# A two-level fast matmul with Gelu, 4096 x 4096 x 4096: more products split a second time, A staged in longer runs and weighed on the way

## The chip, the core and the metric

One NeuronCore of a Trainium2 chip. TensorE multiplies, VectorE (DVE) adds and transposes, ScalarE (ACT) copies out of PSUM, squares and applies Gelu, GpSimd (POOL) and SyncE (SP) issue the transfers. The metric is device time in microseconds; before the change the median of three runs is 1574.81 us (1572.47 to 1576.79).

## The reference

```python
def setup_inputs():
    m, k, n = 4096, 4096, 4096
    return {"a": np.random.randn(m, k).astype(np.float32),
            "b": np.random.randn(k, n).astype(np.float32)}

def reference(a, b):
    x = np.matmul(a, b)
    return 0.5 * x * (1 + np.tanh(np.sqrt(2 / np.pi) * (x + 0.044715 * x**3)))
```

## The kernel before

The product is made by a scheme of Strassen's kind. A, B and the output are cut into quadrants "11", "12", "21", "22" of 2048 x 2048, the operands are converted to 16 bit while they are loaded, and seven products M1 to M7 of sums of quadrants stand for eight. A group is one block of 512 rows of each A half (mb) with one block of 512 columns of each B half (nb): 16 groups, 0 to 15, four to each mb, each of 7 products of 64 matmuls (128 x 128 by 128 x 512). A's block changes during groups 3, 7 and 11. In the first six groups ("raw") B is loaded from the input (converted on the way) and its sums are kept in DRAM (`k_M`); later groups fetch those, in units of 1 MB, into a ring of 8 places in SBUF (`bK`). Group 0 does the first half of K with eight plain products, since nothing else is loaded yet.

Products, and the second level: a "split" product is itself cut into quarters and made of seven quarter products of 256 columns (112 narrow matmuls in place of 64 wide ones). Two consecutive products are split together, with their quarter products interleaved (`PAIR`). Quarter sums of B are made once by VectorE and kept in DRAM (`k_split`); those of A are made when needed, from block sums (`aD`).

```python
PRODUCTS = [
    ("M3", "Y", "11", ("12", "22", 1)),
    ("M5", "X", ("11", "12", -1), "22"),
    ("M7", "X", ("12", "22", -1), ("21", "22", 1)),
    ("M1", "X", ("11", "22", -1), ("11", "22", -1)),
    ("M4", "X", "22", ("21", "11", 1)),
    ("M2", "Y", ("22", "21", -1), "11"),
    ("M6", "Y", ("21", "11", -1), ("11", "12", 1)),
]
...
FRESH = [PRODUCTS[k] for k in (0, 1, 2)] + [
    ("M2", "Y", ("21", "22", -1), "11"), PRODUCTS[3], ("M4", "Y", "22", ("21", "11", 1)),
    ("M6", "X", ("21", "11", -1), ("11", "12", 1)),
]
NP = len(PRODUCTS)
QPH = 4
...
MAKES = (("M3", (1, 0)), ("M5", (2, 1)), ("M1", (4, 0)), ("M2", (5, 3)))
M3_M5, M2_M1 = 0, 3
PLACE = {"M3": (M3_M5, 0), "M5": (M3_M5, 1), "M2": (M2_M1, 0), "M1": (M2_M1, 1)}
SPLIT_AHEAD = 6
FETCH_AHEAD = 12
SPLITS = {M3_M5: (11, 13, 14, 15), M2_M1: (13, 14)}
LOAD_AHEAD = 6
CHECK_GROUP = 9

TURNS = ((2, 2), (3, 3), (5, 2), (6, 2), (8, 0), (9, 0), (10, 2), (11, 2))
```

`SPLITS` says which groups split the pair that begins at product 0 (M3 and M5) and at product 3 (M2 and M1). `FRESH` is the order of products of groups that split the second pair. `TURNS` are the steps at which the staged chunks of the next A block are transposed.

Staging of A: `load_a` fetches a chunk into one of two `stage` buffers, `turn_a` transposes it on VectorE into `aT`, `weigh_rows` sums the squares of its rows on ScalarE. These sums (and those of B, from `square`) decide at the end whether the 16-bit scheme stands or a general path must run. Block 0 of A is loaded a second time, around groups 9 to 12, for its sums alone.

```python
    def load_a(mb, quad, c, h=None):

        ih, kh = int(quad[0]) - 1, int(quad[1]) - 1
        n = NX if h is None else NX // 2
        x = 0 if h is None else h * n
        x0 = (ih * MH + mb * TM) // Q + x
        if not h:
            s = pool.tile([P, NX, RUN], F16, name="stage", tag="stage", bufs=2)
            staged[mb, quad, c] = s
        s = staged[mb, quad, c]
        return [
            (s[g * Q : (g + 1) * Q, x : x + n, :], a_v[kh * CH + c, g, :, x0 : x0 + n, :])
            for g in range(4)
        ]

    def turn_a(mb, quad, c, h=None):
        if not h:
            t = pool.tile([P, NJ // 2, TM * 2], F16, name="aT", tag=f"aT{a_slot[quad]}{c}")
            a_tiles[mb, quad, c] = t
        s, t = staged[mb, quad, c], a_tiles[mb, quad, c]
        x = slice(0, NX) if h is None else slice(h * NX // 2, (h + 1) * NX // 2)
        src = s.bitcast(U32).rearrange("p mb (jj q) -> p jj mb q", q=Q)
        dst = t.bitcast(U32).rearrange("p jj (mb q) -> p jj mb q", q=Q)
        nc.vector.transpose(dst[:, :, x, :], src[:, :, x, :])
        if h != 0 and mb == 0:
            del staged[mb, quad, c]
...
    def weigh_rows(mb, quad, c, xs):

        ih, kh = int(quad[0]) - 1, int(quad[1]) - 1
        s = staged[mb, quad, c]
        if (mb, ih) not in weighed:
            weighed[mb, ih] = pool.tile([P, 2 * CH, NX], F32, name="rows", tag="rows")
        if xs[0] == 0:
            weighed[mb, quad, c] = pool.tile([P, RUN], BF16, name="scrap", tag="scrap")
        for x in xs:
            k = kh * CH + c
            nc.scalar.activation(
                weighed[mb, quad, c][:, :RUN], s[:, x, :], ACT.Square, accum_out=weighed[mb, ih][:, k, x : x + 1]
            )
        if xs[-1] == NX - 1:
            del weighed[mb, quad, c], staged[mb, quad, c]

    def weigh_half(mb, ih):
        k, t = next(checks["a"]), weighed.pop((mb, ih))
        nc.vector.tensor_reduce(
            out=stats["a"][:, k * NX : (k + 1) * NX],
            in_=t.rearrange("p k x -> p x k"), axis=AX.X, op=ALU.add,
        )
...
    def stage_block(mb, turns, turned=True):
        def do(n, fn, *args):
            before.setdefault(n, []).append((fn, args))

        free_at = [0, 0]
        for (quad, c), n in zip(chunks, turns):
            do(max(n - LOAD_AHEAD, free_at.pop(0)), load, (load_a, (mb, quad, c)))
            free_at.append(n + 4)
            if turned:
                do(n, turn_a, mb, quad, c)
            for x in range(3):
                do(n + 1 + x, weigh_rows, mb, quad, c, list(range(NX))[x * 6 : (x + 1) * 6])
            if c == CH - 1 and quad in ("12", "21"):
                do(n + 4, weigh_half, mb, int(quad[0]) - 1)

    for gi in range(len(groups) - 1):
        if groups[gi + 1][0] != groups[gi][0]:
            stage_block(groups[gi + 1][0], [step_number(gi, s, q) for s, q in TURNS])
    stage_block(0, [first_step[CHECK_GROUP] + 8 + 6 * x for x in range(len(chunks))], turned=False)
```

What happens to a finished product, in normal order (`keep` is an ACT copy from PSUM, `tt` a VectorE operation on two tiles, `emit` the Gelu and the output transfer, `new_y` one of five buffers):

```python
        elif name == "M1":
            post["x1", i] = keep("x1", X, RT)
            later.append((gi, i))
        elif name == "M4":
            if not end:
                emit(gi, i, 0, 0, new_y(), X)
            x1 = post["x1", i]
            tt(x1, X, x1, ALU.add)
        elif name == "M2":
            y = new_y()
            tt(y, post.pop(("x1", i)), Y, ALU.subtract)
            if gi:
                flush()
            waiting.append((gi, i, 1, 0, y, y))
        elif name == "M6":
            y = new_y()
            tt(y, Y, post.pop(("x7", i)), ALU.add)
            flush()
            waiting.append((gi, i, 1, 1, y, y))
```

The plan of a split group (cut):

```python
            block = q in SPLIT and not isinstance(oa, str)
            if block and q == PAIR[0][1]:
                places[s] = [ring_place(n, SPLIT_AHEAD, (gi, s, c)) for c in range(CH)]
                users[s] = []
                e = max(ready, last_a, *(e for _, e in places[s]))
                for c, (x, _) in enumerate(places[s]):
                    task(e, open_block, gi, s, c, x)
                for qq in range(QPH):
                    task(e, block_sum, gi, s, oa, qq)
                last_a = e
            o = SPLIT[q][1] if q in SPLIT else oa
            e = n
            if not isinstance(o, str):
                ahead = SPLIT_AHEAD if q in SPLIT else AHEAD
                only = any(n - ahead <= x <= n for x in makes) or made and q not in SPLIT
                tag = "aS" if only or n_a % 2 else "bS"
                n_a += 1
                e = max(n - ahead, ready, last_a, free[tag][-AHEAD - 1] + 1)
                assert e <= n, steps[n]
                free[tag].append(n)
                last_a = e
                task(e, operand_a, gi, s, q, tag)
```

Of the kernel before, what the change touches and what calls it, by code (L numbers as in the profile page):

```python
# [16 lines left out]
P = 128  # L17
Q = 32
# [27 lines left out]
]  # L46
NP = len(PRODUCTS)
# [15 lines left out]

MAKES = (("M3", (1, 0)), ("M5", (2, 1)), ("M1", (4, 0)), ("M2", (5, 3)))
M3_M5, M2_M1 = 0, 3
PLACE = {"M3": (M3_M5, 0), "M5": (M3_M5, 1), "M2": (M2_M1, 0), "M1": (M2_M1, 1)}
SPLIT_AHEAD = 6
FETCH_AHEAD = 12
SPLITS = {M3_M5: (11, 13, 14, 15), M2_M1: (13, 14)}
LOAD_AHEAD = 6  # L70
CHECK_GROUP = 9

TURNS = ((2, 2), (3, 3), (5, 2), (6, 2), (8, 0), (9, 0), (10, 2), (11, 2))
# [8 lines left out]
N_PLAIN = 2 * len(PLAIN)  # L82
N_WARM = 46
# [48 lines left out]
def half_path(  # L132
# [26 lines left out]
    checks = {which: iter(range(stats[which].shape[1] // NX)) for which in stats}  # L159

    a_v = a.rearrange("(x mm) (c g r) -> c g mm x r", mm=Q, g=4, r=RUN)
    b_v = b.rearrange("(c g jj q e) n -> c g e q jj n", g=4, q=Q, e=2, jj=NJ // 2)
# [6 lines left out]
    def load_a(mb, quad, c, h=None):  # L169
# [5 lines left out]
        if not h:  # L175
# [4 lines left out]
            (s[g * Q : (g + 1) * Q, x : x + n, :], a_v[kh * CH + c, g, :, x0 : x0 + n, :])  # L180
# [3 lines left out]
    def turn_a(mb, quad, c, h=None):  # L184
        if not h:
            t = pool.tile([P, NJ // 2, TM * 2], F16, name="aT", tag=f"aT{a_slot[quad]}{c}")
            a_tiles[mb, quad, c] = t
        s, t = staged[mb, quad, c], a_tiles[mb, quad, c]
        x = slice(0, NX) if h is None else slice(h * NX // 2, (h + 1) * NX // 2)
        src = s.bitcast(U32).rearrange("p mb (jj q) -> p jj mb q", q=Q)  # L190
        dst = t.bitcast(U32).rearrange("p jj (mb q) -> p jj mb q", q=Q)
        nc.vector.transpose(dst[:, :, x, :], src[:, :, x, :])  # L192
        if h != 0 and mb == 0:
            del staged[mb, quad, c]

    def load_b(nb, quad, c, h=None):
        kh, jh = int(quad[0]) - 1, int(quad[1]) - 1
        n0 = jh * NH + nb * NC
        if not h:
# [5 lines left out]
            (t[g * Q : (g + 1) * Q, e::2, :], b_v[kh * CH + c, g, e, :, :, n0 : n0 + NC])  # L205
# [23 lines left out]
    def weigh_rows(mb, quad, c, xs):  # L229

        ih, kh = int(quad[0]) - 1, int(quad[1]) - 1
        s = staged[mb, quad, c]
        if (mb, ih) not in weighed:
            weighed[mb, ih] = pool.tile([P, 2 * CH, NX], F32, name="rows", tag="rows")
        if xs[0] == 0:
            weighed[mb, quad, c] = pool.tile([P, RUN], BF16, name="scrap", tag="scrap")
        for x in xs:
            k = kh * CH + c
            nc.scalar.activation(  # L239
                weighed[mb, quad, c][:, :RUN], s[:, x, :], ACT.Square, accum_out=weighed[mb, ih][:, k, x : x + 1]  # L240
            )
        if xs[-1] == NX - 1:
            del weighed[mb, quad, c], staged[mb, quad, c]

    def weigh_half(mb, ih):
        k, t = next(checks["a"]), weighed.pop((mb, ih))
        nc.vector.tensor_reduce(
            out=stats["a"][:, k * NX : (k + 1) * NX],
            in_=t.rearrange("p k x -> p x k"), axis=AX.X, op=ALU.add,
        )  # L250

# [16 lines left out]
    def weigh():  # L268

        for half in sorted(energy):  # L270
            k, t = next(checks["b"]), energy[half]
# [27 lines left out]
    def verdict(row):  # L299

        t = pool.tile([P, RUN], BF16, name="verdict", tag="scrap").bitcast(F32)[0:1, :]
# [30 lines left out]
    def product(gi, s):  # L332
        if gi == len(groups) - 1:
            return LAST[s]
        return (FRESH if gi in SPLITS[M2_M1] else PRODUCTS)[s]
# [59 lines left out]

    N_RAW = NNB + 2
    last_raw = {nb: max(g for g in range(N_RAW) if groups[g][1] == nb) for nb in range(NNB)}
    maker = {nb: min(g for g in range(N_RAW, len(groups)) if groups[g][1] == nb) for nb in range(NNB)}
# [145 lines left out]
    later = []  # L544

    def combine():
# [5 lines left out]
        later.clear()  # L552

# [13 lines left out]
    def settle(gi, name, i):  # L567

        X, Y = banks.get(("X", i)), banks.get(("Y", i))
        end = gi == len(groups) - 1  # L570
# [19 lines left out]
        elif name == "M4":  # L590
# [3 lines left out]
            tt(x1, X, x1, ALU.add)  # L594
        elif name == "M2":
            y = new_y()
# [448 lines left out]
```

## Time and profile before

| | us |
|---|---|
| median of three runs | 1574.81 |
| span of the profiled run | 1572.0 |
| TensorE busy | 1553.1 |
| VectorE busy | 1112.0 |
| ScalarE busy | 670.1 |
| row sums of A on ScalarE (512 squares and 512 reads of the accumulator) | 212.8 + 95.6 |
| sums of A and of kept B on VectorE (`aS`, 188 and 112 of them) | 223.2 + 133.8 |
| 1 MB unit of kept B, issue to landing (median) | 11.5 |

A line of a timeline gives the start, the duration, the engine, the line of the kernel, the operation with what it writes and reads, and how many were merged; in brackets the idle time ahead of it and what ended that. The durations of matmuls overlap[...]: the difference of two starts is the time that TensorE spent. A named releaser that was done long before is not the cause; then the engine's own queue has to be followed.

### The profile page before, as it was taken

How to read it: one execution, taken by the hardware profiler on the slowest of the kernel's cores; microseconds unless marked ns; L12 is line 12 of the kernel's file. 1: busy time of each engine (PE TensorE's matmuls, PEld its weight loads, DVE VectorE, ACT ScalarE, POOL GpSimd, SP SyncE). 2: the span in 40 equal slices, each digit the busy share in tenths (PEclk: the TensorE clock that was granted, in tenths of full speed). 3: DMA queues.
4: the chain of work that ended last, by engine and by line, in shares of the span. 5: the costliest groups of instructions: out<-in, count | busy, mean ns of one | idle time of the engine just before them, and what ended most of it. 6: DMA issues, size and time to landing. Idle time of an engine off the chain costs nothing. (4 is left out here: it accounts for less than half of the span.)

```text
span 1572.0 us, 21821 instructions
## 1 busy us (share of the span) xinstructions
PE 1553.1 (99%) x7822; PEld 766.1 (49%) x7822; DVE 1112.0 (71%) x1281; ACT 670.1 (43%) x1670; POOL 391.2 (25%) x682
## 2 busy tenths in 40 slices
PE   9999999999999999999999999999899999999998
PEld 4444444444444444444444444444644457677653
DVE  1697988969888886776755557577654668688853
ACT  1036444338874641212566345563356733232211
POOL 7763433331124300011222112121222111212100
PEclk9999999999999999999999999999999999999999
DMA  9999999994799986799999789998999856978852
GB/s 175 197 217 296 265 318 268 287 201 79 202 228 294 296 321 243 306 324 315 330 339 302 229 277 332 354 353 270 365 279 291 229 173 239 322 257 296 297 211 82
DMA packets 219780, 418.88 MB, mean 266 GB/s; under 512 B 18192, under 2 KB 141072, under 8 KB 200464
## 3 DMA queue, kind: packets, MB, share of 16 engines
q0 software_dynamic: 157024, 249.60, 66.5%
q1 hardware_dynamic: 62640, 167.81, 28.5%
q8 instruction: 63, 1.03, 0.3%
q14 instruction: 53, 0.43, 0.1%
HBM read 333.45 MB, written 167.78 MB: 319 GB/s over the span
## 5 line engine op out<-in xcount | busy, mean ns | idle before, releaser
L418 PEld LDWEIGHTS <-aS 128*128 128x128 f16 x4448 | 435.5, 98 | 533.8 <-issue 7.1
L418 PE MATMUL accX<-bK,aS 128*128 128x512 f16 x1664 | 362.9, 380 | 4.0 <-ACT x L529 4.0
L418 PEld LDWEIGHTS <-aT 128*128 128x128 f16 x1728 | 169.1, 98 | 205.1 <-issue 1.8
L832 DVE TENSOR_TENSOR aS<-aT 128x2048 f16<-128x2048 f16 x188 | 223.2, 1217 | 58.2 <-PE accX L418 47.1
L239 ACT ACTIVATE scrap<-stage 128x256 bf16<-128x256 f16 x512 | 212.8, 416 | 50.1 <-DMA stage<-in_a_dram 35.6
L556 ACT ACTIVATE y<-y 128x512 f32<-128x512 f32 x192 | 119.0, 630 | 270.0 <-DVE y L565 269.9
L217 POOL DMA_DIRECT2D bR<-in_b_dram x320 | 173.2, 543 | 208.5 <-DMA bR<-in_b_dram 117.7
L418 PE MATMUL accY<-bK,aS 128*128 128x512 f16 x1024 | 222.3, 379 | 0.0
L818 POOL DMA_DIRECT2D bK<-k_M x116 | 62.5, 541 | 449.3 <-PE accX L418 121.8
L217 POOL DMA_DIRECT2D stage<-in_a_dram x176 | 111.6, 640 | 240.2 <-ACT scrap L239 188.7
L378 DVE TENSOR_TENSOR aS<-aT 128x2048 f16<-128x2048 f16 (+1 forms) x112 | 133.8, 1199 | 32.3 <-PE accX L418 23.4
L418 PE MATMUL accX<-bS,aS 128*128 128x512 f16 x704 | 153.4, 379 | 1.9 <-DVE bS L378 1.2
L378 DVE TENSOR_TENSOR bS<-bR 128x2048 f16<-128x2048 f16 x110 | 133.6, 1217 | 18.0 <-PE accX L418 9.6
L261 ACT ACTIVATE square<-bR 128x1024 bf16<-128x1024 f16 x120 | 123.0, 1049 | 50.5 <-DVE energy L565 50.3
L529 ACT COPY x<-accX 128x512 f32<-128x512 f32 x120 | 69.5, 586 | 153.4 <-PE accX L418 147.3
L529 ACT COPY m<-accX 128x512 f32<-128x512 f32 x68 | 39.2, 582 | 187.1 <-PE accX L418 175.3
L192 DVE STREAM_TRANSPOSE aT<-stage 128x2048 uint32<-128x2048 uint32 (+1 forms) x37 | 74.5, 2017 | 62.6 <-DMA stage<-in_a_dram 56.5
L832 DVE TENSOR_TENSOR bS<-bK 128x2048 f16<-128x2048 f16 x80 | 96.9, 1216 | 28.6 <-DMA k_split<-bS 28.6
L418 PE MATMUL accY<-bK,aT 128*128 128x512 f16 x512 | 111.8, 379 | 0.0
L418 PE MATMUL accX<-bK,aT 128*128 128x512 f16 x512 | 111.8, 379 | 0.0
L500 PEld LDWEIGHTS <-aS 128*128 128x128 f16 x960 | 93.9, 98 | 17.2 <-issue 2.5
L239 ACT ACTIVATION_READ_ACCUMULATOR scrap<-stage 128x1 f32 x512 | 95.6, 187 | 0.0
(70 smaller groups left out, 1302.9 us busy)
## 6 DMA issues: line engine op xcount, KB each, us to landing
bK<-k_M POOLq DMA_DIRECT2D x116, 1024.0 KB, 11.5
out_dram<-y SPq DMA_DIRECT2D x256, 256.0 KB, 6.6
bR<-in_b_dram POOLq DMA_DIRECT2D x320, 128.0 KB, 7.7
k_M<-bS SPq DMA_DIRECT2D x80, 512.0 KB, 6.7
k_split<-bS SPq DMA_DIRECT2D x80, 512.0 KB, 7.7
stage<-in_a_dram POOLq DMA_DIRECT2D x144, 256.0 KB, 12.3
bK<-k_split POOLq DMA_DIRECT2D x18, 1024.0 KB, 6.6
k_M<-bR SPq DMA_DIRECT2D x16, 1024.0 KB, 12.2
```

Source lines behind the costliest of these rows:

```text
L192: nc.vector.transpose(dst[:, :, x, :], src[:, :, x, :])
L217: nc.gpsimd.dma_start(out=dst, in_=src)
L239: nc.scalar.activation(weighed[mb, quad, c][:, :RUN], s[:, x, :], ACT.Square, accum_out=weighed[mb, ih][:, k, x : x + 1])
L261: nc.scalar.activation(t[:, :], src, ACT.Square)
L378: nc.vector.tensor_tensor(out=x, in0=y, in1=z, op=ALU.add if o[2] > 0 else ALU.subtract)
L418: nc.tensor.matmul(acc[:, :], sa[:, j // 2, i * P : (i + 1) * P, j % 2], sb[:, j, :], start=start and j == 0, stop=stop and j == 3, skip_g ...
L500: nc.tensor.matmul(banks[chain, i][:, :] if wide else out, sa[:, j // 2, r * P : (r + 1) * P, j % 2], sb[:, : NC] if wide else sb[:, j * N ...
L529: nc.scalar.copy(out=t[:, :], in_=src[:, :])
L556: nc.scalar.activation(y[:, :], src[:, :], ACT.Gelu_apprx_tanh)
L818: nc.gpsimd.dma_start(out=t, in_=kept_unit(*key[1:])[:, :])
L832: nc.vector.tensor_tensor(out=t, in0=y, in1=z, op=ALU.add if op > 0 else ALU.subtract)
```

## The change

The change does these things:

- Three more pairs are split: (M3, M5) in groups 9 and 10 also, and (M2, M1) in group 15 also. So groups 9, 10, 11, 13, 14, 15 have split pairs, and 13, 14, 15 have two.
- A is loaded in runs of 512 elements instead of 256 (`load_half`: half the rows, both chunks of K), so that one ScalarE instruction weighs 512 elements. The squares are written over the staged row itself.
- Block 0 is weighed during groups 0 to 2, from the staging of the first loads, and not loaded again.
- In groups 7 and 11, where A's block changes and B comes from DRAM, the products run in the order M3, M5, M7, M6, M1, M4, M2 (`TURNING`). A12 is then used last by M7 and A11 by M1, so the next A11 and A12 can be put in their places sooner. M6 is then settled together with M2.
- The squares of nb 3's B blocks (groups 3 and 4, A changes in 3) are spread thinly (`TWO_GROUPS`).
- The last sums are written into the `x1` and `x7` tiles rather than into new `y` tiles.
- Quarter sums of B are made at other places, some in groups that work on another nb (`MAKES`), and the block sums of A are planned by a count of VectorE's work per step; those of M1 and M2 are kept from group 13 to 15, M2's in the `stage` buffers.

The diff, cut to its core:

```diff
+TURNING = [PRODUCTS[k] for k in (0, 1, 2, 6, 3, 4, 5)]
...
-MAKES = (("M3", (1, 0)), ("M5", (2, 1)), ("M1", (4, 0)), ("M2", (5, 3)))
 M3_M5, M2_M1 = 0, 3
 PLACE = {"M3": (M3_M5, 0), "M5": (M3_M5, 1), "M2": (M2_M1, 0), "M1": (M2_M1, 1)}
+
+
+MAKES = (
+    (6, 1, 0, 1, "M3"), (6, 2, 1, 1, "M5"), (6, 3, 2, 3, "M3"), (6, 4, 3, 3, "M5"),
+    (8, 2, 2, 2, "M3"), (8, 4, 0, 2, "M5"), (8, 5, 1, 2, "M1"),
+    (9, 2, 0, 0, "M3"), (9, 3, 1, 0, "M5"), (9, 4, 2, 3, "M1"), (9, 5, 3, 3, "M2"),
+    (10, 2, 0, 2, "M2"), (10, 4, 0, 0, "M1"), (10, 5, 3, 0, "M2"),
+)
+STAY = ("M2", "M1")
+STAY_AHEAD = 20
+BLOCK_AHEAD = 12
 SPLIT_AHEAD = 6
 FETCH_AHEAD = 12
-SPLITS = {M3_M5: (11, 13, 14, 15), M2_M1: (13, 14)}
+SPLITS = {M3_M5: (9,10,11,13,14,15), M2_M1: (13,14,15)}
 LOAD_AHEAD = 6
-CHECK_GROUP = 9
-
-TURNS = ((2, 2), (3, 3), (5, 2), (6, 2), (8, 0), (9, 0), (10, 2), (11, 2))
+
+TURNS = ((2, 2), (3, 2), (4, 2), (5, 2), (6, 2), (7, 2), (9, 0), (10, 2))
+RAW_TURNS = ((2, 2), (3, 2), (5, 2), (6, 1), (7, 1), (8, 1), (10, 1), (11, 1))
 
 
 
...
     ("22", "21", "12", True), ("22", "22", "22", True),
 ]
 N_PLAIN = 2 * len(PLAIN)
+
+TWO_GROUPS = [x // 2 for x in range(16)] + [8 + 2 * x for x in range(16)]
...
+    def load_half(mb, quad, h):
+
+        ih, kh = int(quad[0]) - 1, int(quad[1]) - 1
+        n = NX // 2
+        x0 = (ih * MH + mb * TM) // Q + h * n
+        s = pool.tile([P, NX, RUN], F16, name="stage", tag="stage", bufs=2)
+        s = staged[mb, quad, h] = s.rearrange("p (x c) r -> p x (c r)", c=CH)
+        return [(s[g * Q : (g + 1) * Q, :, :], a_v[kh, g, :, x0 : x0 + n, :]) for g in range(4)]
+
+    def turn_half(mb, quad, h):
+        for c in range(CH):
+            turn_a(mb, quad, c, h)
 
...
+    def weigh_row(dst, src):
+
+        nc.scalar.activation(src, src, ACT.Square, accum_out=dst)
+
...
+        return (TURNING if gi >= N_RAW and groups[gi + 1][0] != groups[gi][0] else PRODUCTS)[s]
...
+        for gi, i, Y in last:
+            y = post.pop(("x7", i))
+            tt(y, Y, y, ALU.add)
+            flush()
+            waiting.append((gi, i, 1, 1, y, y))
+        last.clear()
...
+        elif name == "M6" and product(gi, NP - 1)[0] == "M2":
+            return
         elif name == "M2":
-            y = new_y()
-            tt(y, post.pop(("x1", i)), Y, ALU.subtract)
+            if product(gi, NP - 1)[0] == "M2":
+                last.append((gi, i, Y))
+            y = post.pop(("x1", i))
+            tt(y, y, Y, ALU.subtract)
             if gi:
                 flush()
             waiting.append((gi, i, 1, 0, y, y))
         elif name == "M6":
-            y = new_y()
-            tt(y, Y, post.pop(("x7", i)), ALU.add)
+            y = post.pop(("x7", i))
+            tt(y, Y, y, ALU.add)
             flush()
             waiting.append((gi, i, 1, 1, y, y))
 
...
+        (0, "A11_0 B12_0 T11_0 W11_0 B11_0 A21_0 A12_0 B22_0 B21_0"),
+        (4, "T21_0 W21_0 A22_0"),
+        (6, "T12_0 W12_0"),
...
+        (16, "T12_1 W12_1:0-4"),
+        (17, "W12_1:4-16 A21_1"),
...
+        (34, "W22_1:0-1"),
+        (35, "W22_1:1-2"),
...
+        for (quad, h), n in zip(halves, turns(gi)):
+            at_step(max(n - LOAD_AHEAD, free_at.pop(0)), load, (load_half, (mb, quad, h)))
+            free_at.append(n + 5)
+            at_step(n, turn_half, mb, quad, h)
+            for x in range(4):
+                at_step(n + 1 + x, weigh_rows, mb, quad, h, list(range(NX // 2))[x * NX // 2 // 4 : (x + 1) * NX // 2 // 4])
+            if h and quad in ("12", "21"):
+                at_step(n + 5, weigh_half, mb, int(quad[0]) - 1)
...
+    def plan_block(gi, s, n):
+
+        mb, (name, _, oa, _) = groups[gi][0], product(gi, s)
+        twins = [g for g in SPLITS[PLACE[name][0]] if groups[g][0] == mb and g >= gi]
+        last = n
+        if name in STAY:
+            last = step_number(twins[-1], s, PAIR[-1][1])
+        first = max(n - (STAY_AHEAD if name in STAY else BLOCK_AHEAD), ready(mb, oa))
+        if name == "M2":
+            places = []
+            first = max(first, turned[mb, "21"] + 3)
+        else:
+            got = [ring_place(n, n - first, (gi, s, c)) for c in range(CH)]
+            places = [x for x, _ in got]
+            first = max(first, *(e for _, e in got))
+        for x in places:
+            ring_end[x] = last
+        for c in range(CH):
+            task(first, open_block, gi, s, c, places[c] if places else None)
+        e = first
+        for q in range(QPH):
+            e = sum_step(n, e)
+            task(e, block_sum, gi, s, oa, q)
+        for g in twins if name in STAY else (gi,):
+            blocks[g, s] = places, e
+            if g != gi:
+                for c in range(CH):
+                    task(first, same_block, gi, g, s, c)
```

## The prediction, made before the changed kernel was run

> **What bounds the kernel now.** I read the engines' shares first, then TensorE's timeline from its first matmul to its last, looking for the places where it stands still, and then the other engines around each of those.
>
> ```profile
> PE 1553.1 (99%) x7822; PEld 766.1 (49%) x7822; DVE 1112.0 (71%) x1281; ACT 670.1 (43%) x1670; POOL 391.2 (25%) x682
> ```
>
> TensorE is busy for 99% of the span, the next engine for 71%. Time can change only through the number of TensorE cycles or through the stops in the last per cent. From TensorE's timeline, two plain products and then the ends of a split pair (M3 and M5 of group 13):
>
> ```profile
> 343.32 27.79 PE L418 MATMUL accX<-bS,aS 128*128 128x512 f16 x128
> 370.95 13.98 PE L418 MATMUL accX<-bS,aT 128*128 128x512 f16 x64
> ...
> 1290.25 3.87 PE L500 MATMUL accY<-bK,aS 128*128 128x512 f16 x32
> 1293.96 1.91 PE L500 MATMUL accY<-bK,aT 128*128 128x256 f16 x16
> ...
> 1315.13 13.98 PE L418 MATMUL accX<-bK,aS 128*128 128x512 f16 x64
> ```
>
> Starts count, not durations. 128 matmuls of 512 columns take 370.95 - 343.32 = 27.63 us (215.9 ns each); the same two products, split, take 1315.13 - 1290.25 = 24.88 us. A split pair saves 2.75 us.
>
> All of TensorE's stops after the warm-up add up to 12.2 us: 0.60 at 35 us, 1.44 at 113, 1.51 at 128, 0.58 at 157, 0.39 at 399, 0.62 at 448, 0.68 at 456, and two in group 11, the first split group, where A's block also changes:
>
> ```profile
> 1095.11 1.91 PE L500 MATMUL accY<-bK,aT 128*128 128x256 f16 x16
> 1099.39 3.87 PE L500 MATMUL accX<-bK,aS 128*128 128x512 f16 x32 [2.36 <-DVE y L565]
> ...
> 1118.81 13.98 PE L418 MATMUL accX<-bK,aS 128*128 128x512 f16 x64
> 1136.79 15.48 PE L418 MATMUL accX<-bK,aS 128*128 128x512 f16 x64 [4.01 <-ACT x L529]
> 1152.12 13.98 PE L418 MATMUL accX<-bK,aT 128*128 128x512 f16 x64
> ```
>
> The named releaser of the 4.01 us is an ACT copy long done. VectorE's timeline shows the real one: the sums for M1 stand behind a transpose of A11 that waits for its transfer.
>
> ```profile
> 1120.94 2.35 DVE L832 TENSOR_TENSOR aS<-aT 128x2048 f16<-128x2048 f16 x2
> 1133.12 2.31 DVE L192 STREAM_TRANSPOSE aT<-stage 128x2048 uint32<-128x2048 uint32 x1 [9.82 <-DMA stage<-in_a_dram]
> 1135.35 4.59 DVE L832 TENSOR_TENSOR aS<-aT 128x2048 f16<-128x2048 f16 x4
> ```
>
> The product after the stop takes 15.3 us from start to start in place of 13.81: the trace has the clock at half for 3.4 us there. Group 11 runs from 1091.41 to 1193.56, 102.15 us; a group with one split pair and no stops should take 7 x 13.81 - 2.75 = 93.9 us. So 8.2 us are lost in it.
>
> [...]
>
> **The change, part by part.**
> - Splits. Pairs (M3, M5) are split in groups 9, 10, 11, 13, 14, 15 in place of 11, 13, 14, 15; pairs (M2, M1) in 13, 14, 15 in place of 13, 14. Nine pairs for six: 3 x 2.75 = **-8.25 us** on TensorE, unhidden because TensorE is the path.
> - What a pair costs others. M3 needs 5 quarter sums of A where it needed none, M5 4 block sums and 5 quarter sums where it needed 4: 10 x 1.22 = 12.2 us of VectorE, and 16 joins at 0.42 = 6.7 us; 8 ACT copies at 0.376 = 3 us. VectorE is busy for 58.1 us in 883 to 980 (group 9) and 62.3 of 97 in 980 to 1077 (group 10): with 19 more, 77 to 81 of 94, about 84%. In 1276 to 1368, with both pairs split, it is at 73.1 of 92 without one stop. In 14 and 15 the blocks of M1 and M2 are kept, 8 sums (9.7 us) fewer each. Beside other work: 0.
> - Group 11 (and 7). In the new order A12 and A11 are free after M7 and M1, so their successors land in those places without holding the group's later sums; block sums are looked for up to 12 steps ahead and spread, in place of 4 in one go before the 2.36 us stop. I count 80 to 90% of the 7.9 us (2.36 + 4.01 + 1.5 of half clock): **-6.7 us**.
> - Group 3 and 4. Stops of 0.39, 0.62 and 0.68. ACT, at 75.0 of 97 us in 399 to 496, gets 64 row sums of 512 in place of 128 of 256 (0.54 us each from start to start); half of nb 3's squares come in every other step. **-1 us**.
> - y written into x1 and x7. VectorE waits 3.88 us at 119.34 for an output transfer before it can have a y buffer; then bS is late and TensorE stops for 1.51 at 128.48. With fewer y buffers asked for, **-1.5 us**.
> - Block 0 weighed in group 0. ACT gets 128 row sums, 16 of them 8.6 us per chunk, written over the staged rows: so each waits for the transpose, and the next transfer into that buffer waits for ACT. Up to 60 us this just fits: W11_0 from 13.5 (end of its transpose) to 22.1, and the buffer is asked for at 22.64; W12_0 to about 45.6, asked for at 45.69. Then it does not fit:
>
> ```profile
> 70.15 1.15 POOL L217 DMA_DIRECT2D stage<-in_a_dram  x2 [1.05 <-DMA stage<-in_a_dram]
> 71.94 3.77 POOL L217 DMA_DIRECT2D stage<-in_a_dram  x6 [0.63 <-DMA stage<-in_a_dram]
> ```
>
> This is A22 of the second half of K, into the buffer of A11. A11's transpose is 63.18 to 65.49, so its weighing runs to 65.5 + 8.6 = 74.1, 4 us after 70.15. Its landing (5.7 us median there) then comes at about 82 and 85 for its halves, where VectorE transposes them at 78.67 and 81.27. M7, which starts at 83.76 on TensorE, needs the second half from 85.5 on and would get it at about 87.6 to 89. **+3 us** (0 to 5).
> - Reloading block 0 for its check falls away (8.4 MB landed in groups 9 to 12, 77 us of ACT); the splits ask 3 units of 1 MB more per pair (7 for 4) and making quarter sums of a B block that the group does not use about 10 more. Hidden in the plan: 0, but see below.
> - The end. Group 15 ends with M6, whose last tile needs a VectorE sum (0.69) before the Gelu; now the Gelu reads M7 directly. **+0.7 us**.
> - New small stops in 9, 10, 15, not placed: **+2 us**.
>
> Sum: -8.25 - 6.7 - 1 - 1.5 + 3 + 0.7 + 2 = -11.75. From 1574.8 this is **1563 us**.
>
> **The rivals.** (1) Transfers become the wait. DMA is at 0.98 to 1.12 of its share in groups 9 and 10, a unit of 1 MB takes 11.5 us (median) to land, and a split pair eats one every 24.88 / 7 = 3.6 us; the kept block of M1 holds 2 of the 8 places from group 13 to 15. Against it: 13 and 14, with both pairs split, run without a stop. If wrong, 2 to 4 us in each of three to five groups, some with a half clock of 1.5: 1570 to 1580. (2) The weighing at the start holds A's staging more than I reckon, each chunk pushing the next while VectorE has no idle time (39.7 of 40 us in 80 to 120): +6 to +8 and a half clock: 1568 to 1570. (3) VectorE bounds the new split groups: 84% busy with in-order waits. Stops of about 2 us per pair as at 1099: 1569. (4) All is hidden and the start is neutral: -8.25 - 7.9 - 1.7 - 1.5 gives 1555.
>
> **Range and chances.** The three runs of before lie within 4.3 us. The sure term is -8.25, the likely one -6.7; the start and new stops can take it back. 1556 to 1571 should hold it 8 times in 10. 2% is 31.5 us, more than any single term: faster by over 2% 0.02, within 2% 0.95, slower 0.03 (late transfers in several groups).
>
> **What would show it.** TensorE's matmuls: a split product has 112 in place of 64, so 96 more for each of 3 pairs, 8110. Pairs of 24.9 us in nine places. Group 11 near 94 us with no half clock. M7 of group 0 starting its third row late, near 87. No VectorE wait on an output transfer at 120. I am wrong if groups 9 and 10 exceed 95 us each, if group 7 or 11 still waits for staged A, or if group 1 starts more than 6 us after 119.9.

## The result, and the profile after

The changed kernel takes 1615.34 us (median of four runs, 1610.52 to 1619.63) against 1573.64 (1570.95 to 1576.79) for the kernel before. The ratio is 1.0263, 95% interval 1.0228 to 1.0299: slower by 2.6%, where I had said 1563, and 0.03 for slower by over 2%.

The profile page of the changed kernel, part 1, busy time of each engine and its share of the span (1614.2 us, before 1572.0):

```profile
PE 1560.9 (97%) x8110; PEld 796.7 (49%) x8110; DVE 1136.8 (70%) x1357; ACT 600.6 (37%) x1322; POOL 384.9 (24%) x682
```

TensorE is busy for 7.8 us *more*, with narrower matmuls that should take 8.25 us less, and its share has fallen to 97%. VectorE's share has not grown. So TensorE works slower in places (its mean granted clock is 0.987, before 0.998) and stands still longer; no other engine has become full.

Where that is, the starts of the matmuls tell. The time of a group is the difference between the first matmuls of two successive groups; without any stop it is 7 x 13.81 = 96.7 us, 93.9 with one split pair, 91.2 with two.

| group | before | after | without stops (after) |
|---|---|---|---|
| 0 and 1 | 205.1 | 211.4 | - |
| 2, 3, 4, 5 | 96.7, 97.2, 98.3, 96.7 | 96.7, 96.7, 99.7, 96.7 | 96.7 each |
| 6 | 96.7 | **107.9** | 96.7 |
| 7, 8 | 96.7, 96.7 | 96.7, 98.3 | 96.7 each |
| 9, 10 | 96.7, 96.7 | **106.8, 102.0** | 93.9 each |
| 11 | 102.1 | **109.6** | 93.9 |
| 12 | 96.7 | 98.0 | 96.7 |
| 13, 14, 15 | 91.2, 91.2, 94.1 | 91.2, 91.2, 91.4 | 91.2 each |

All stops of TensorE together, with some 1.4 us of the warm-up, are 13.6 us before and 47.3 after: +33.7. After some of them the granted clock is 0.50: in eight stretches of 3.41 to 10.24 us, 41.0 us together, and in one of 3.41 us before. Taking the starts against 13.81 us a product, that costs 16.4 us after and 1.5 before: +14.9. The splits give back 8.25 and the tail costs 0.8, which makes +41 of the 42.2 us between the two profiled spans.

**Group 6**, the plainest case: it splits nothing and A does not change in it; it only makes quarter sums of B for later groups. TensorE's timeline there (line 456 is a plain product, 538 a split one, 609 the sums of finished products, 919 the sums of A, the block sums and the quarter sums):

```profile
684.14 13.98 PE L456 MATMUL accY<-bK,aS 128*128 128x512 f16 x64
...
706.42 16.73 PE L456 MATMUL accY<-bK,aS 128*128 128x512 f16 x64 [8.30 <-DVE x L609]
722.99 13.98 PE L456 MATMUL accY<-bK,aT 128*128 128x512 f16 x64
```

It stands for 8.30 us, and the product after that takes 722.99 - 706.42 = 16.57 us in place of 13.81 (the granted clock is 0.50 from 701.79 to 712.03). It waits for VectorE to clear accY. VectorE's timeline in the same place:

```profile
692.11 1.22 DVE L919 TENSOR_TENSOR aS<-aT 128x2048 f16<-128x2048 f16 x1
...
703.41 1.23 DVE L919 TENSOR_TENSOR bS<-bK 128x2048 f16<-128x2048 f16 x1 [10.08 <-DMA k_split<-bS]
704.55 1.22 DVE L919 TENSOR_TENSOR aS<-aT 128x2048 f16<-128x2048 f16 x1
705.68 2.48 DVE L609 TENSOR_TENSOR x<-x,accY 128x512 f32<-128x512 f32 x4
```

VectorE is not busy: it stands for 10.08 us at a quarter sum that needs a `bS` buffer, and the buffer's last content is still on its way to DRAM (`k_split<-bS`). The sums for TensorE stand behind it: their product is over at 698.12 us on TensorE (684.14 + 13.98), and they start at 705.68, after the quarter sum. The store in question was issued at 687.61 us and landed at 703.31; SyncE, which issues the stores, had issued four output transfers just ahead of it (683.37 to 685.01), and these landed between 693.95 and 701.38. The waits of that kind, from VectorE's list of waits (total us, times, longest), in the kernel before:

```profile
DVE bS L832 <- DMA k_split<-bS: 28.6, 10, 6.2
```

and in the changed kernel:

```profile
DVE bS L919 <- DMA k_split<-bS: 56.3, 17, 10.1
```

There were such waits before, of up to 6.2 us, and they were covered: before, TensorE has no stop of half a microsecond or more from group 5 to group 10.

**Group 9** has it twice, beside a split pair (TensorE, changed kernel):

```profile
996.07 8.39 PE L456 MATMUL accY<-bK,aS 128*128 128x512 f16 x32 [3.55 <-DVE aS L919]
...
1009.63 15.33 PE L456 MATMUL accY<-bK,aS 128*128 128x512 f16 x64 [5.18 <-DVE x L609]
1024.80 3.87 PE L538 MATMUL accY<-bK,aS 128*128 128x512 f16 x32
```

**Group 11** was to lose its stops and has more of them (TensorE, changed kernel):

```profile
1168.25 15.67 PE L456 MATMUL accY<-bK,aS 128*128 128x512 f16 x64 [2.55 <-DVE aS L919]
1186.02 15.68 PE L456 MATMUL accX<-bK,aS 128*128 128x512 f16 x64 [2.09 <-DVE aS L919]
1207.42 15.42 PE L456 MATMUL accX<-bK,aT 128*128 128x512 f16 x64 [5.72 <-ACT x L567]
```

VectorE's timeline shows all three behind transposes of the next A block, each waiting for its staged rows:

```profile
1164.71 2.37 DVE L209 STREAM_TRANSPOSE aT<-stage 128x1024 uint32<-128x1024 uint32 x2 [7.37 <-DMA stage<-in_a_dram]
1167.01 4.59 DVE L919 TENSOR_TENSOR aS<-aT 128x2048 f16<-128x2048 f16 x4
...
1182.48 2.37 DVE L209 STREAM_TRANSPOSE aT<-stage 128x1024 uint32<-128x1024 uint32 x2 [10.88 <-DMA stage<-in_a_dram]
...
1203.11 2.37 DVE L209 STREAM_TRANSPOSE aT<-stage 128x1024 uint32<-128x1024 uint32 x2 [13.74 <-DMA stage<-in_a_dram]
```

It is the picture from before (a transpose waiting 9.82 us, TensorE 4.01), three times over.

**The start** has a new stop in group 1, with a half clock after it (0.50 from 159.07 to 165.90; 96 matmuls in 23.38 us in place of 20.7); TensorE, changed kernel:

```profile
160.48 23.54 PE L456 MATMUL accX<-bS,aS 128*128 128x512 f16 x96 [3.89 <-DVE bS L418]
183.86 13.98 PE L456 MATMUL accX<-bS,aT 128*128 128x512 f16 x64
```

VectorE's sum that it waits for, itself waiting for a chunk of B:

```profile
159.20 1.23 DVE L418 TENSOR_TENSOR bS<-bR 128x2048 f16<-128x2048 f16 x1 [5.38 <-DMA bR<-in_b_dram]
```

### The profile page after: what moved, and what is told of

Its sections match the earlier page's. It is cut to its first block, busy times and chain, and to the rows that moved or that the text cites. A ratio compares the mean times of both kernels' runs of the same rounds, so it can differ in the third digit from the quotient of the medians.

```text
span 1614.2 us, 22064 instructions
## 1 busy us (share of the span) xinstructions
PE 1560.9 (97%) x8110; PEld 796.7 (49%) x8110; DVE 1136.8 (70%) x1357; ACT 600.6 (37%) x1322; POOL 384.9 (24%) x682
## 4 chain that ended last, share of the span: by engine, by line
PE 68%; DMA 20%; DVE 5%; issue 3%; POOL 3%; ACT 1%; DVEq 0%; POOLq 0%; ACTq 0%
PE accX L456 32%; PE accY L456 23%; DMA stage<-in_a_dram 8%; PE accY L538 7%; DMA k_split<-bS 7%; PE accX L538 7%; DMA bR<-in_b_dram 3%; POOL bR L245 1%; POOL stage L245 1%; DVE bS L919 1%; DVE x L609 1%; DMA bK<-k_M 1%; DMA k_M<-bS 1%; DVE aS L919 1%; DVE bS L418 1%
## 5 line engine op out<-in xcount | busy, mean ns | idle before, releaser
L456 PEld LDWEIGHTS <-aS 128*128 128x128 f16 x4192 | 412.8, 99 | 546.5 <-issue 44.8
L456 PE MATMUL accX<-bK,aS 128*128 128x512 f16 x1536 | 339.2, 383 | 8.1 <-DVE aS L919 7.0
L259 ACT ACTIVATE stage<-stage 128x512 f16<-128x512 f16 (+1 forms) x320 | 169.5, 532 | 152.5 <-DVE aT L209 100.0
L456 PE MATMUL accY<-bK,aS 128*128 128x512 f16 x896 | 202.8, 389 | 21.7 <-DVE x L609 15.6
L600 ACT ACTIVATE x<-x 128x512 f32<-128x512 f32 x128 | 78.2, 627 | 273.3 <-DVE x L609 273.0
L538 PEld LDWEIGHTS <-aS 128*128 128x128 f16 x1440 | 140.9, 98 | 22.1
L418 DVE TENSOR_TENSOR bS<-bR 128x2048 f16<-128x2048 f16 x110 | 133.6, 1218 | 24.3 <-PE accX L456 13.7
L209 DVE STREAM_TRANSPOSE aT<-stage 128x1024 uint32<-128x1024 uint32 (+1 forms) x61 | 76.1, 1278 | 101.9 <-DMA stage<-in_a_dram 100.7
L245 POOL DMA_DIRECT2D stage<-in_a_dram x144 | 84.4, 593 | 179.3 <-ACT stage L259 126.8
L919 DVE TENSOR_TENSOR bS<-bK 128x2048 f16<-128x2048 f16 x70 | 84.5, 1220 | 56.3 <-DMA k_split<-bS 56.3
L609 DVE TENSOR_TENSOR x<-accY,x 128x512 f32<-128x512 f32 x116 | 77.7, 689 | 35.3 <-ACT y L600 24.5
L456 PE MATMUL accY<-bK,aT 128*128 128x512 f16 x448 | 97.8, 379 | 0.0
L609 DVE TENSOR_TENSOR energy<-energy,square 128x1024 bf16<-128x1024 bf16 x120 | 82.3, 685 | 7.3 <-ACT square L299 5.2
```

The source lines that it names most:

```text
L209: nc.vector.transpose(dst[:, :, x, :], src)
L245: nc.gpsimd.dma_start(out=dst, in_=src)
L259: nc.scalar.activation(src, src, ACT.Square, accum_out=dst)
L418: nc.vector.tensor_tensor(out=x, in0=y, in1=z, op=ALU.add if o[2] > 0 else ALU.subtract)
L456: nc.tensor.matmul(acc[:, :], sa[:, j // 2, i * P : (i + 1) * P, j % 2], sb[:, j, :], start=start and j == 0, stop=stop and j == 3, skip_g ...
L538: nc.tensor.matmul(banks[chain, i][:, :] if wide else out, sa[:, j // 2, r * P : (r + 1) * P, j % 2], sb[:, : NC] if wide else sb[:, j * N ...
```

## The experiments

**The theory after the result.** Groups 6, 9 and 10: VectorE fills three `bS` buffers with quarter sums faster than their stores land, and stands in front of TensorE's work. Five of the fourteen makes in `MAKES` are for an nb that their group does not use, so each also fetches two units of 1 MB for that alone. Rivals: VectorE itself is too full for a split pair beside the makes; or the bytes are simply too many for the DMA engines. Group 11: the split pair's units and the staging of A meet in one queue (rival: the new turns are too early). Start: weighing block 0 delays the staging (rival: the new places of `y`).

Group times of the runs that bear on groups 6 to 12 (us), all from the starts of matmuls:

| | 0+1 | 6 | 9 | 10 | 11 | 12 | span |
|---|---|---|---|---|---|---|---|
| before | 205.1 | 96.7 | 96.7 | 96.7 | 102.1 | 96.7 | 1572.0 |
| changed | 211.4 | 107.9 | 106.8 | 102.0 | 109.6 | 98.0 | 1614.2 |
| 1 own_units | 211.9 | 98.8 | 97.2 | 96.4 | 104.2 | 98.2 | 1585.8 |
| 2 five_buffers | 209.4 | 96.7 | 95.0 | 95.9 | 105.9 | 100.9 | 1582.6 |
| 3 later_turns | 209.6 | 106.2 | 109.1 | 96.5 | 99.4 | 104.5 | 1614.2 |
| 4 unweighed | 207.5 | 105.9 | 108.9 | 96.2 | 112.5 | 102.2 | 1612.9 |
| 5 pair_in_12 | 210.3 | 96.7 | 95.0 | 95.0 | 96.7 | 94.8 | 1568.2 |
| 6 new_y | 205.8 | 106.9 | 109.8 | 96.3 | 111.5 | 96.7 | 1609.3 |
| 7 own_makes | 212.0 | 96.7 | 96.7 | 96.7 | 96.7 | 95.3 | 1572.8 |
| 8 start_later | 204.2 | 96.7 | 95.0 | 95.0 | 96.7 | 95.4 | 1561.5 |
| 9 start_later_three | 203.6 | 106.4 | 106.5 | 97.1 | 96.7 | 94.6 | 1584.0 |
| 10 before_12_15 | 207.2 | 96.7 | 96.7 | 96.7 | 96.7 | 99.5 | 1569.5 |

Group 10 of kernels with three buffers and a split pair there moves between 96.2 and 102.0 from trace to trace (changed, 3, 4, 6, 9), so no single value of it is read. The start moves too: six of these kernels have the same one (changed, 1, 2, 3, 5, 7), and its two groups take 209.4 to 212.0 us; the kernel before and run 10 share theirs and take 205.1 and 207.2. Each row is one trace. Runs 1 to 7 and 9 were measured once, and the four times of the changed kernel lie 9.1 us apart, so it is the groups that are compared and not the totals.

**1. Units that the group has anyway.** The quarter sums for a foreign nb are made from other units, those of the group's own nb that it fetches for its own products: ten fetches of 1 MB fewer, as many sums and stores. The sums are of other data than the reference needs, so this is a run for its time only.

```diff
-    plan_fetch(units, (gi, *make[:2], c), n, FETCH_AHEAD)
+    plan_fetch(units, (gi, nb, near, c), n, FETCH_AHEAD)
-    blocks = [split_tiles[gi, nb, name, c] for c in range(CH)]
+    blocks = [split_tiles[gi, groups[gi][1], near, c] for c in range(CH)]
```

> The changed kernel, but quarter sums of a B block that the group does not use are made from the units that the group has fetched anyway: as many sums and stores, ten fetches of 1 MB fewer, in groups 6, 9 and 10 (the sums are those of other data). Theory, the transfer queue is full there and VectorE stands behind late stores: group 6 falls from 107.9 us to 97 to 99, group 9 from 106.8 to 97 to 101, group 10 from 102.1 to 97 to 100; in all about 1596 us. Rival, the extra VectorE work of splits and quarter sums: within 3 us of the changed kernel, 1612 to 1618.

Measured 1587.66 us (before beside it 1577.1). Groups 6, 9 and 10 together fall from 316.7 to 292.4 us, 24.3 of the 32.2 us that they had lost; 6 and 9 alone, which repeat well, give back 18.7 of 24.1. VectorE's waits for a `bS` buffer fall from 56.3 to 37.1 us, and the latest store of group 6 lands after 11.8 us in place of 16.6. As many sums and stores are made as before, so the fetches are what makes the stores late enough to hurt.

**2. Five buffers, the same traffic.** Half of the quarter sums in groups 6, 9 and 10 are put into the `stage` buffers, so that five are in turn where three were. What is fetched, summed and stored stays as it is.

```diff
+    n_made[0] += 1
+    if gi in (6, 9, 10) and n_made[0] % 2:
+        t = pool.tile([P, NX, RUN], F16, name="bS", tag="stage", bufs=2)
+        t = t.rearrange("p x r -> p (x r)")[:, : 4 * NC]
+    else:
         t = pool.tile([P, 4 * NC], F16, name="bS", tag="bS", bufs=AHEAD + 1)
```

> The changed kernel, but every second quarter sum of B in groups 6, 9 and 10 goes to one of the two staging buffers of A, idle there: five buffers in place of three between VectorE and the stores, the same transfers. If the wait is only a short burst that three buffers cannot cover: groups 6, 9 and 10 fall to 97 to 99 each, 1596 us. If the queue is full over the whole group: the stop moves to the fetched units or remains, at most 5 us gained, 1610. Rival, VectorE's own work: no change, 1615.

Measured 1584.13 us (before 1577.1). Groups 6, 9, 10: 96.7, 95.0, 95.9, within 3.1 us of no loss at all; 6 and 9 give back 23.0 of 24.1. VectorE's waits for a buffer, in this run:

```profile
DVE bS L919 <- DMA k_split<-bS: 11.5, 5, 3.5
```

The view of the 20 stores issued in group 6 has as its last line the time from issue to landing, in the changed kernel

```profile
DMA to landing us min/median/max: 2.6/8.3/16.6
```

and with five buffers

```profile
DMA to landing us min/median/max: 2.6/11.0/17.1
```

The stores land *later*, and nobody is hurt. The stretches of group 6 say the same of the rate (stretch, length, busy time and count of PE, PEld, DVE, ACT, POOL, granted clock, DMA share, GB/s), first the changed kernel:

```profile
615.07:722.99 107.92, 99.61 (x450) 44.53 (x448) 62.02 (x65) 16.36 (x28) 8.94 (x17) 0.95 0.82 321
```

then five buffers:

```profile
614.10:710.80 96.70, 96.70 (x450) 43.83 (x449) 62.33 (x65) 16.42 (x28) 8.93 (x17) 1.00 0.84 335
```

65 instructions and 62 us of VectorE in both, and the transfers run at 335 GB/s where they ran at 321. Both rivals fall for these groups: neither VectorE's work nor the number of bytes was the limit by itself, but how many quarter sums may be under way at once while stores land that late.

**3. Later turns.** The turns of before with the new order of products.

```diff
-TURNS = ((2, 2), (3, 2), (4, 2), (5, 2), (6, 2), (7, 2), (9, 0), (10, 2))
+TURNS = ((2, 2), (3, 3), (5, 2), (6, 2), (8, 0), (9, 0), (10, 2), (11, 2))
```

> The changed kernel with A's staged halves of groups 7 and 11 transposed at the steps of the kernel before, one half to each 1 to 1.5 products in place of one to each product. Theory, staging at one half per product asks the queue for more than it moves: group 11 falls from 109.6 us to 97 to 102, group 12 stays within 98; 1603 to 1608 in all. Rival, group 11 inherits a queue already full from the split pair and the makes: 107 or more, and group 12 gets longer.

1615.85 us (before 1577.1). Group 11 gains 10.2 us, to 99.4, as the theory had it, but group 12, which was to stay within 98, loses 6.5, and group 8 goes from 98.3 to 108.0: most of the wait is moved into the next group, where the same transposes now stand. So later turns help group 11 and are no cure.

**4. Block 0 not weighed.** No row sums of block 0 are taken; its entries in the table are filled with a constant, so the check of A that decides on the general path is left out for that block.

```diff
-    before.setdefault(n, []).append((weigh_first, (what[1:3], int(what[4]), xs)))
+    nc.vector.memset(stats["a"][:, :], 256.0)
```

> The changed kernel without the weighing of A's block 0 (its row sums are replaced by a constant). Theory, the weighing holds the staging buffers at the start: group 0 falls from 108.1 us to 106 and group 1 from 103.4 to 99 or below, 1608 in all. Rival, the squares of B or the buffers of the output do it: groups 0 and 1 unchanged, 1615.

1614.79 us (before 1577.1), and not the 1608 of the theory. The start falls by 3.9 us against the changed kernel, 1.9 to 4.5 against the six traces with its start, and a stop of 2.68 us stays near 158. Weighing is part of the start's loss, and no part of what matters in groups 6 to 12.

**5. The pair of group 11 in group 12.** Run 2, and the first pair split in 12 in place of 11, where no A block changes and as many pairs are split in all.

```diff
-SPLITS = {M3_M5: (9,10,11,13,14,15), M2_M1: (13,14,15)}
+SPLITS = {M3_M5: (9,10,12,13,14,15), M2_M1: (13,14,15)}
```

> Five buffers for the quarter sums of B, and the split pair of group 11, where A's block changes, moved to group 12: the same work. Theory, group 11 loses time because the split pair's seven units and the staged A meet in one queue (units landed after 20 us there): group 11 falls from 105.9 us to 97 to 99 and group 12 from 100.9 to 94 to 97, 1570 in all. Rival, the staging of A alone fills the queue of group 11: 102 or more in group 11, 1578.

1569.82 us (before 1573.92). Groups 11 and 12 take 96.7 + 94.8, against 109.6 + 98.0: no stop is left in 11 (TensorE, this run):

```profile
1096.92 13.98 PE L456 MATMUL accY<-bK,aT 128*128 128x512 f16 x64
1110.73 27.79 PE L456 MATMUL accX<-bK,aS 128*128 128x512 f16 x128
1138.36 13.98 PE L456 MATMUL accY<-bK,aS 128*128 128x512 f16 x64
```

The staged rows of A in group 11, from issue to landing, in the changed kernel:

```profile
DMA to landing us min/median/max: 11.3/18.0/21.3
```

and with the pair in 12:

```profile
DMA to landing us min/median/max: 3.9/10.1/13.0
```

Run 2, which has the five buffers too, has a median of 18.1 us, so the buffers are not what does it. With three fetched units fewer in the group (a split pair takes 7 where two plain products take 4) A arrives in little more than half the time. But GpSimd also asks for it sooner: the first staged rows are issued 1.1 us after the group's start (1098.05), in the changed kernel 15.4 us after it (1142.23). No run separates the faster landing from the earlier request; asking earlier with the pair left in 11 was not tried.

**6. New `y` tiles again**, in place of the sums written into x1 and x7.

```diff
-    y = post.pop(("x1", i))
-    tt(y, y, Y, ALU.subtract)
+    y = new_y()
+    tt(y, post.pop(("x1", i)), Y, ALU.subtract)
```

(and the same for x7.)

> The changed kernel with the last sums written to y buffers of their own again. By the prediction's term the wait for an output transfer near 120 us and the TensorE stop of 1.5 us after it come back: +1.5 us in group 1. Rival, TensorE waits for B's transfers in group 1 either way and the later stop near 160 us shrinks by as much: groups 0 and 1 together unchanged within 1 us.

1610.9 us (before 1573.92). VectorE's wait for the output transfer is back, and TensorE's stop behind it. VectorE:

```profile
124.76 0.69 DVE L609 TENSOR_TENSOR y<-accY,x 128x512 f32<-128x512 f32 x1 [3.81 <-DMA out_dram<-y]
```

TensorE:

```profile
130.03 7.07 PE L456 MATMUL accY<-bS,aT 128*128 128x512 f16 x32 [2.12 <-DVE bS L418]
```

Yet the stop near 160 and its half clock are gone, and groups 0 and 1 take 205.8 us in place of 211.4. Both the theory (1.5 us more) and its rival (no change) are wrong. The stop near 160 is 3.64 to 4.26 us long in all six traces with the changed start, so its absence here is no chance: the part of the change that removes a stop of some 2 us brings a larger one 30 us later.

**7. Quarter sums made only where they are at hand.** Three buffers, no split in 9, 10 and 11, the first pair in 12, and every make in a group that works on that nb.

```diff
-    (6, 1, 0, 1, "M3"), (6, 2, 1, 1, "M5"), (6, 3, 2, 3, "M3"), (6, 4, 3, 3, "M5"),
-    ...
+    (6, 1, 0, 1, "M3"), (6, 2, 1, 1, "M5"),
+    (8, 1, 0, 2, "M3"), (8, 2, 1, 2, "M5"), (8, 4, 0, 2, "M1"), (8, 5, 3, 2, "M2"),
+    (9, 1, 0, 3, "M3"), (9, 2, 1, 3, "M5"), (9, 4, 0, 3, "M1"), (9, 5, 3, 3, "M2"),
+    (10, 1, 0, 0, "M3"), (10, 2, 1, 0, "M5"), (10, 4, 0, 0, "M1"), (10, 5, 3, 0, "M2"),
```

> The changed kernel without the split pairs of groups 9 and 10 and with the pair of 11 in 12, so that every quarter sum of B is made in a group that fetches that block anyway, 10 or 20 to a group at the steps of the kernel before; three buffers. Theory, it is the fetches for blocks that the group does not use, on top of a split pair's, that make the stores late: groups 6, 9 and 10 run in 97 to 98 us, 1573 in all. Rival, 20 quarter sums in a group with three buffers stop it by themselves: 100 or more in 9 and 10.

1574.36 us (before 1575.22). Groups 6, 9, 10 and 11 are at 96.7 each with three buffers, and the waits for a buffer fall to 19.0 us. Groups 9 and 10 make 20 quarter sums each, so that number does not stop a group by itself; nor does it in the kernel before, which makes about 20 in groups 6, 9 and 10. (Group 6 makes only 10 here.) Without the foreign makes and the split pairs beside them three buffers are enough; but then the sums for a split in 9 and 10 are not there in time.

**8. A version that puts these together.** Run 5, and the second half of K of A11 and A12 is not weighed in group 0 but loaded once more in group 2 (244.6 to 252.9 us) and weighed from there into group 3, two rows a step. The squares of nb 3 end sooner, in group 3 (not in the lines shown).

```diff
-        (14, "T11_1 W11_1 A22_1 B11_1"),
-        (16, "T12_1 W12_1:0-4"),
-        (17, "W12_1:4-16 A21_1"),
+        (14, "T11_1 A22_1 B11_1"),
+        (16, "T12_1 A21_1"),
...
+        (67, "A11_1"),
+        (69, "A12_1"),
+        (73, "W11_1:0-2"),
...
+        (88, "W12_1:14-16"),
```

> As the run with the pair in 12, but chunks A11 and A12 of the second half of K are not weighed in group 0: they are loaded again and weighed in group 2, where A's staging buffers are free; and the squares of nb 3 end in group 3. Theory: group 0 back to 106 to 107, group 1 to 100 to 101 (as without weighing), group 4 to 98 to 100: 5 us below the run with the pair in 12, about 1565, which is faster than the kernel before by 0.5%. Rival, the start waits for transfers whatever is weighed: no gain, 1570.

1563.68 us (median of four, 1562.07 to 1566.2), ratio to before 0.9936, interval 0.9917 to 0.9956: 0.6% faster than the kernel before, a small gain but clear of the noise, and 3.2% faster than the changed kernel. The start goes from 210.3 (run 5) to 204.2, and the stop near 160 from 3.95 us to 0.54. Its page:

```profile
PE 1544.9 (99%) x8110; PEld 793.1 (51%) x8110; DVE 1135.8 (73%) x1357; ACT 600.6 (38%) x1322; POOL 390.6 (25%) x690
```

The same 8110 matmuls as the changed kernel, in 16.0 us less of busy time: that is the half clock gone (the mean granted clock is 1.000, in the changed kernel 0.987), which I had put at 16.4 from the starts.

**9. The same with three buffers**, to size the buffers alone.

```diff
-        if gi in (6, 9, 10) and n_made[0] % 2:
+        if False:
```

> The run with the later weighing, with three buffers in place of five for the quarter sums of B. Theory: groups 6, 9 and 10 are back at 106 to 108, 105 to 109 and 96 to 102 us, 1585 to 1592 in all. Rival, the start alone set how full the queue was later: 1565 to 1570.

1585.94 us (before 1575.22). The span is 22.5 us longer than that of run 8, with groups 6 and 9 back at 106.4 and 106.5 us. TensorE in group 9:

```profile
1000.29 15.66 PE L456 MATMUL accY<-bK,aS 128*128 128x512 f16 x64 [4.80 <-DVE x L609]
1015.79 3.87 PE L538 MATMUL accY<-bK,aS 128*128 128x512 f16 x32
```

**10. The kernel before, with the pair of 11 in 12 and the second pair split in 15 too**, and nothing else of the change; the order and the ending of group 15 follow.

```diff
-SPLITS = {M3_M5: (11, 13, 14, 15), M2_M1: (13, 14)}
+SPLITS = {M3_M5: (12, 13, 14, 15), M2_M1: (13, 14, 15)}
```

> The kernel before with two edits alone: the split pair of group 11 moved to group 12, and the pair (M2, M1) of group 15 split. Theory: group 11 falls from 102.1 us to 96.7 to 98, group 12 from 96.7 to 94 to 95, group 15 from 94.1 to 91.4: 9 to 10 us below the kernel before, 1564. Rival, the three buffers for quarter sums or the ring stop it in 12 or 15: 1570 or above.

1570.95 us (median of 20 runs), ratio 0.9978, interval 0.9971 to 0.9985. Group 11 has no loss (96.7), 15 goes from 94.1 to 91.9, but 12 takes 99.5: a transpose of A that now falls between the joins of the split pair puts 2.3 us in front of them. TensorE:

```profile
1211.73 4.56 PE L502 MATMUL accY<-bK,aS 128*128 128x256 f16 x25 [3.77 <-DVE accY L516]
```

VectorE:

```profile
1207.92 2.30 DVE L192 STREAM_TRANSPOSE aT<-stage 128x2048 uint32<-128x2048 uint32 x1
...
1211.25 0.75 DVE L516 TENSOR_TENSOR accY<-join,accY 128x256 f32<-128x256 f32 x2
```

So the old loss of group 11 (8.2 us) was the meeting of split and staging, and goes without the new order of products; but 5.6 us of it come back in 12 (99.5 against 93.9), which I had not expected. The rival had 1570 or above, and for another reason.

## Why the prediction was wrong

- **The step that failed** is "Reloading block 0 for its check falls away ...; the splits ask 3 units of 1 MB more per pair (7 for 4) and making quarter sums of a B block that the group does not use about 10 more. Hidden in the plan: 0, but see below". It should have been some 30: groups 6, 9 and 10 lose 11.2 + 12.9 + 8.1 = 32.2 us against their times without stops (25.5 to 28.5 in the other four traces with three buffers and the same makes, runs 3, 4, 6 and 9). I counted the ten fetches rightly and asked only whether the *fetched* units would be late. What was late were the stores beside them, in groups that I did not look at (6) or looked at for their busy time (9, 10). Runs 1, 2 and 9 show it: with ten fetches fewer, 24.3 us come back; with two buffers more and the same bytes, 29.1 (groups 6, 9 and 10 of run 2); and, in the best version, three buffers in place of five cost 22.5 us.
- **It could have been read in advance.** The list of VectorE's waits of the kernel before has the line with 28.6 us and a longest wait of 6.2. My prediction looked only at stops of TensorE; a wait of VectorE, with sums for TensorE behind it, is slack already spent. How much was left the list does not say: in run 1 a wait of 6.3 us in group 10 is followed by a stop of 0.35 us, and one of 4.4 us in group 6 by a stop of 1.96.
- **"Group 11: -6.7 us"** was +7.5. The mechanism that I had read in the profile (sums behind a transpose that waits for its transfer) was right; that freeing A12 and A11 early would cure it was wrong. Their places were not what was late: the staged rows were asked for 15.4 us into the group and took 18.0 us to land; with the pair in 12 it is 1.1 and 10.1 (run 5). The cure was to take the split pair, with its three extra units, out of the group.
- **"Splits: -8.25 us, unhidden"** held: a split pair takes 24.88 us in groups 9, 10 and 11 of the changed kernel too, 13, 14 and 15 take 91.2, 91.2, 91.4, and run 8 has 9, 10 and 12 at 95.0, 95.0, 95.4 against 93.9. In the changed kernel 64 narrow matmuls take 6.98 us from start to start (1035.71 to 1042.69), 109 ns each, about half of the 215.9 of a wide one.
- **"Beside other work: 0"**, what a pair costs the other engines, nearly held for VectorE: run 2 has the work of the change and no stop of 1 us in 9 or 10. It was 1.1 to 2.0 us a group.
- **Start: "-1.5" for y in x1 and x7, "+3" for weighing.** The measured total is +6.3 us (2.2 to 6.9 over the traces with the two starts). The stop at 128 did go (it comes back in run 6, with the wait of 3.81 us), but a stop of 3.89 us at 160 more than took its place, so that this part, meant to gain 1.5, costs 5.6 in all (211.4 - 205.8; 3.6 to 6.2 over the six traces). Weighing is worth 3.9 (run 4), within what I gave it, but this is luck: the 3 us were to be a stop in M7 of group 0 at 85 to 89, and there TensorE stands for 0.38 + 0.40 us (0.34 in run 4). The rows of block 0 are 256 wide and take 0.40 us each from start to start, so that a chunk is weighed in 6.4 us and not in 8.6. Of the 3.9 us, 1.4 lie in group 0 and 2.5 in group 1. The two costs do not simply add: with either part gone the stop at 160 is smaller, by 1.2 us or the whole.
- **"Group 3 and 4: -1"** was +0.9: group 3 gained 0.5, and 4 lost 1.4 with stops of 0.63 and 1.52 at 444 and 451, whose cause stays open. The other traces with this start (1, 2, 3, 5, 7) have 100.8 to 101.6 in group 4, so the term was nearer to +2 or +3.
- **"The end: +0.7"**: from TensorE's last matmul to the end, 5.2 before, 6.0 after. **"New small stops: +2"**: 1.6 in group 8 and 1.3 in 12.
- **The rivals.** "Transfers become the wait" was the right one, with the wrong transfer and too small: 2 to 4 us in each of three to five groups, where 8 to 13 came in three and 16 in group 11 (in this trace; group 10 mostly loses 2 to 3). I sized it from what a late unit costs, and left out that a late store holds up VectorE (10.08 us in group 6) and the sums that stand behind it, and that the half clock adds 14.9 us to 33.7 of stops. "The start: +6 to +8" was near at +6.3 in size, but not by the weighing alone, since the places of `y` weigh as much (run 6). "VectorE bounds the split groups" fell with run 2.
- My range of 15 us rested on the spread of the kernel before and on TensorE's fixed work. It should have been wide on one side: the plan had 11.75 us to gain, and taking out its ten fetches for foreign blocks alone brings back 24.3 us of its loss (run 1). Of the signs that I had named for being wrong, two came: groups 9 and 10 exceed 95 us, and group 11 still waits for staged A. Group 1 starts at 121.9, within the 6 us that I had allowed.

**What stays open.** The order in which transfers arrive in group 1, and so why `y` in x1 and x7 brings the stop near 160 rather than another; whether four buffers would do as well as five (not tried); what part of a store's delay comes from the output transfers that SyncE issues ahead of it; whether A asked for earlier would cure group 11 with the pair in it; the stops of 1.77 us at 115 and of 1.52 at 451; why group 10 differs from trace to trace with three buffers.

## What to carry to other kernels

As an estimate, a producer that stores its results needs buffers for as long as a store takes to land *under load*, divided by the time between two results, and one for the result in work. It is worked out from group 6 of run 2: 20 stores between 618.4 and 692.7 us are one in 3.9 us, the latest takes 17.1 us to land, so 4 to 5 are under way at worst. Only three and five buffers were tried. Count them before adding traffic, and read the waits of the engines that the bounding one waits for, not only its own stops. When fetches and staging meet in one group, move one of them to a group where it is alone before changing the order of work. When a plan adds transfers, ask which waits already in the profile they will lengthen, and who stands behind the engine that waits.

## What the runs showed of the hardware that was not expected

- The half clock came after shorter stops than the one of 4.01 us in the kernel before. In group 11 of the changed kernel the product after a stop of 2.55 us and the one after 2.09 us last 15.67 and 15.68 us in place of 13.98. After 2.36 us (the kernel before, at 1099) and after 2.12 us (run 6, at 130, where the next 32 matmuls take 7.07 us as elsewhere) there is no such loss. So the half clock came once after a stop of 2.09 us and not after one of 2.36: the length of a stop alone did not decide it. What else did was not shown.
- Between the first product and the last matmul, the granted clock is 0.50 in eight stretches of the changed kernel and in one of the kernel before. They last 3.41, 6.83 or 10.24 us. Here is the stop of 2.09 us in the first line, and the half clock in the second (in the columns given for group 6, the third number from the end is the granted clock):

```profile
1183.08:1186.49 3.41, 1.32 (x7) 0.44 (x6) 3.41 (x4) 1.60 (x5) 0.70 (x2) 1.00 1.09 271
1186.49:1189.91 3.42, 3.42 (x10) 1.18 (x9) 2.88 (x3) 3.40 (x12) 0.17 (x1) 0.50 1.26 211
```

and the kernel before, with the stop of 2.36 us across both lines and a granted clock of 1.00 in each:

```profile
1095.51:1098.92 3.41, 1.51 (x14) 1.21 (x13) 3.41 (x5) 0.75 (x2) 3.36 (x5) 1.00 0.76 219
1098.92:1102.33 3.41, 2.94 (x26) 2.44 (x26) 3.34 (x7) 2.86 (x7) 1.07 (x3) 1.00 0.88 261
```

- With five buffers the stores of group 6 land later (median 11.0 against 8.3 us) while the transfers of the group run no slower (335 against 321 GB/s): a longer time to land was hardly a loss, since VectorE had buffers left to go on with.
